# A hybrid S5, conformer and ConvFFN step on one core: an own list scheduler, and split weights kept in DRAM

## The chip, the core and the metric

The kernel runs on one core of a Trainium2 chip. The core has TensorE (PE; its weight loads are shown apart as PEld), VectorE (DVE), ScalarE (ACT), GpSimd (POOL) and SyncE (SP, which here only issues DMAs), each with an in-order stream of instructions of its own, and 16 DMA engines that move data between DRAM and SBUF. TensorE writes its products to PSUM, and DVE and ACT bring them out. The metric is the device time of one execution in microseconds (us).

## The reference, cut to what matters

A prompt of 2048 tokens and 8 single-token samples with carried state go through one layer:

```
h = RMSNorm(x); p = h @ w_in                        # 1024 -> 1536
s: S5 scan of p[:, :512], GELU, s * sigmoid(s @ w_glu)
c: p[:, 512:1024] * sigmoid(p[:, 1024:]), causal conv of 31 taps, LayerNorm, swish
x = x + RMSNorm(concat(s, c) @ w_out)
h = RMSNorm(x); u = conv3(h @ w_up)                 # 1024 -> 5632, three taps over positions
x = x + RMSNorm((silu(u_gate) * u_val) @ w_down)    # 2816 -> 1024
```

Everything is float32. The outputs are the new x and the new states.

## The kernel before, in words

Tokens are cut into six tiles of 344 (the last one is 328 and the 8 samples), and a tile's activations lie as 128 channels by 344 tokens. Two tiles make a **round**; there are three rounds (0, 1, 2), and each goes through all weights. A weight **block** is 8, 6 or 4 chunks of 128 x 128: 12 blocks of w_in (`in`), 2 of w_glu and 8 of w_out (`out`), 44 of w_up, 32 of w_down with 4 chunks and 8 of w_down with 6 chunks (`ffn`). That is 106 different blocks, used 326 times, since in the last piece of round 2 the 8 blocks of 6 chunks are read once for each of its two tiles. A number behind a name in this text is that of the round or tile; `ORDER` has the stages: in 0, in 1, a third of in 2, out 0, the rest of in 2, ffn 0, out 1, the last piece of ffn 0, ffn 1, out 2, the last piece of ffn 1, ffn 2, the last piece of ffn 2. That last piece is the 8 blocks of 6 chunks; behind out 1 and out 2 it is what TensorE can do while the norms of the next round are worked out.

For float32 accuracy each operand is split in two: H is the value in the type fp32r, L the rest of it. A product is three matmuls, W_H h_H, W_H h_L and W_L h_H (`group`). There are 12672 of them, with output `ps`, called the **main matmuls** below. A block comes from DRAM into `wraw` (`w_load_to`, L327, on SP's queue), then ACT writes `wh` (its H) and POOL writes `wlo`, wraw minus wh (`w_split_to`, L337). Each of the three tiles has three buffers (`NRAW`, `NW`). This is done for all 326 uses.

Beside the main matmuls run **tasks**, written as generators: the set-up of the S5 matrices (DVE work on tile `wk`), the S5 scan (steps on DVE in tiles ST and UR; round 0 has two, UR00 and UR016, of 16 channel groups each, and `CR` takes a scan's last state), the conv of 31 taps (DVE steps `acc<-c,V,acc`; the first 128 channels on POOL, in `cacc`), and the norms between stages (tiny matmuls `trp<-col_d,sqs` sum squares, a chain of tiny DVE steps on tile `st` takes the square root, `trp<-ident,st` turns the result back, and eight channel blocks are then scaled and added, in tiles mx and y). The **auxiliary matmuls** of the tasks, with output `trp`, stand in the same PE stream as the main ones. `split_h` makes the two halves of h that a stage reads.

The order of the program text is set by simple clocks (`clk`) that pace the tasks against the main matmuls, and operations marked "any" go to DVE or POOL by these clocks. The framework's scheduler then sets the order of each engine's stream.

At the start (`prep_first`) the tokens of tile 0 (xa, xb) are squared and summed on ACT (output `xn`), turned on PE, copied to xT, scaled on DVE by the norm and the gain V1 (`xn<-xT,V,trp`) and split into h; then tile 1 likewise.

## Time and profile before

| | |
|---|---|
| median of 3 runs | 2403.68 us (2399.62 to 2403.96) |
| span of the profiled execution | 2398.0 us |
| median minus span | 5.7 us |
| busy: PE, DVE, ACT, POOL | 2215.5, 1692.2, 1026.9, 1085.0 us |
| moved by DMA | 248.60 MB |

The span runs from the first to the last instruction of the profiled execution. The profiled execution is not one of the three that were timed, so the 5.7 us is how its span stands to their median: what lies around the span, and the scatter between executions. Matmuls overlap each other in their records, so PE busy in the whole of a stretch means that it never ran dry there. A windows view cuts the span into stages; a stage's bounds are the times at which its first and last main matmuls run.

### The profile page before, as it was taken

To read this page: it belongs to the slowest core of one execution; us is meant where nothing else is said; L and a number is where in the kernel's file an instruction comes from. 1 tells how busy PE (TensorE), PEld (TensorE's weight loads), DVE (VectorE), ACT (ScalarE), POOL (GpSimd) and SP (SyncE) were. 2 spreads that over 40 slices of the span, in tenths; PEclk is the share of its full clock that TensorE was granted. 3 is DMA by queue.
4 is the path that set the end of the run, shared out by engine and by line. 5 is a ranking of instruction groups with operands and counts; after the bars stand their busy time and mean duration, and the time that the engine had idled before them with its cause. 6 is when DMAs were issued, how large, how long until landed. Compare 5 with 4: busy or idle time off the path is not lost.

```text
span 2398.0 us, 36717 instructions
## 1 busy us (share of the span) xinstructions
PE 2215.5 (92%) x13923; PEld 2185.1 (91%) x13923; DVE 1692.2 (71%) x3156; ACT 1026.9 (43%) x1897; POOL 1085.0 (45%) x708
## 2 busy tenths in 40 slices
PE   8897788979898999999898999999997899999997
PEld 8887788979898899999888999999897899999997
DVE  8979985388789997564799896644549835445464
ACT  5666355344444234454443433345335443233345
POOL 3797443343233334444665434333537533333335
PEclk8998899989999999999999999999998999999999
DMA  7859333352342232142332322323324222222224
GB/s 222 207 146 235 105 112 114 85 140 80 90 127 83 62 86 77 58 146 79 122 133 79 89 60 65 88 91 89 107 88 145 91 64 64 86 62 63 88 84 137
DMA packets 361501, 248.60 MB, mean 104 GB/s; under 512 B 53824, under 2 KB 343352, under 8 KB 357685
## 3 DMA queue, kind: packets, MB, share of 16 engines
q1 hardware_dynamic: 318503, 218.21, 31.6%
q10 hardware_dynamic: 42470, 27.37, 4.3%
q8 instruction: 110, 1.80, 0.3%
q0 software_dynamic: 352, 0.67, 0.1%
q14 instruction: 66, 0.54, 0.1%
HBM read 197.60 MB, written 48.10 MB: 102 GB/s over the span
## 4 chain that ended last, share of the span: by engine, by line
PE 58%; DVE 29%; issue 3%; ACT 3%; DMA 1%; POOL 1%; DVEq 0%; ACTq 0%; SPq 0%; POOLq 0%
PE ps L114 56%; DVE acc L99 7%; DVE ST L82 4%; DVE UR L82 3%; DVE y L82 2%; DVE mx L99 2%; DVE mx L82 2%; PE trp L114 2%; DVE sqs L82 1%; DVE st L99 1%; DVE h L82 1%; DVE xT L99 1%; PE trp L118 1%; DVE s L99 1%; DVE acc L82 1%
## 5 line engine op out<-in xcount | busy, mean ns | idle before, releaser
L114 PE MATMUL ps<-h,wh 128*128 128x346 f32 (+3 forms) x5376 | 1310.3, 326 | 32.3 <-DVE h L82 15.7
L85 POOL TENSOR_TENSOR wlo<-wraw,wh 128x1024 fp32r<-128x1024 f32 (+2 forms) x326 | 672.1, 2063 | 931.9 <-ACT wh L75 888.5
L114 PEld LDWEIGHTS ps<-h,wh 128*128 128x128 f32 x5376 | 947.0, 192 | 39.4 <-DVE h L82 18.9
L114 PE MATMUL ps<-h,wlo 128*128 128x346 f32 (+3 forms) x2688 | 872.2, 325 | 0.0
L114 PE MATMUL ps<-f,wh 128*128 128x344 f32 (+1 forms) x2112 | 511.4, 326 | 10.5 <-DVE acc L99 7.1
L114 PEld LDWEIGHTS ps<-h,wlo 128*128 128x128 f32 x2688 | 514.7, 192 | 0.2
L99 DVE SCALAR_TENSOR_TENSOR acc<-ps,FC,acc 128x344 f32<-128x344 f32 (+1 forms) x528 | 299.9, 569 | 238.3 <-ACT acc L75 232.1
L75 ACT ACTIVATE wh<-wraw 128x1024 fp32r<-128x1024 f32 (+2 forms) x326 | 295.8, 908 | 352.0 <-PE ps L114 236.9
L114 PEld LDWEIGHTS ps<-f,wh 128*128 128x128 f32 x2112 | 372.4, 193 | 12.6 <-issue 10.0
L99 DVE SCALAR_TENSOR_TENSOR acc<-c,V,acc 128x344 f32<-128x344 f32 (+1 forms) x609 | 347.8, 571 | 9.2
L114 PE MATMUL ps<-f,wlo 128*128 128x344 f32 (+1 forms) x1056 | 343.5, 325 | 0.0
L114 PEld LDWEIGHTS ps<-f,wlo 128*128 128x128 f32 x1056 | 203.5, 193 | 0.0
L85 POOL TENSOR_TENSOR f<-acc,f 128x344 fp32r<-128x344 f32 (+1 forms) x101 | 97.4, 966 | 217.5 <-ACT f L75 214.1
L75 ACT ACTIVATE acc<-ps,FC 128x344 f32<-128x344 f32 (+1 forms) x264 | 164.7, 625 | 68.8 <-PE ps L114 65.8
L82 DVE TENSOR_TENSOR y<-y,ps 128x344 f32<-128x344 f32 (+1 forms) x192 | 96.7, 506 | 117.1 <-PE ps L114 116.6
L75 ACT ACTIVATE f<-acc 128x344 fp32r<-128x344 f32 (+1 forms) x132 | 64.3, 488 | 260.1 <-DVE acc L82 260.0
L75 ACT ACTIVATE acc<-acc 128x344 f32<-128x344 f32 (+1 forms) x132 | 64.6, 490 | 243.6 <-DVE acc L99 240.7
L82 DVE TENSOR_TENSOR msq<-msq,sq 128x344 f32<-128x344 f32 (+1 forms) x49 | 58.1, 1191 | 114.5 <-ACT sq L75 114.5
L82 DVE TENSOR_TENSOR acc<-acc,HT 128x8 f32<-128x8 f32 x44 | 65.7, 1492 | 63.2 <-ACT acc L75 57.0
L85 POOL TENSOR_TENSOR cacc<-cacc,wk 128x344 f32<-128x344 f32 x87 | 94.0, 1080 | 27.6 <-ACT wk L75 24.2
L114 PE MATMUL ps<-sHL,wh 128*128 128x344 f32 (+1 forms) x384 | 95.4, 328 | 10.5 <-ACT sHL L75 7.9
L82 DVE TENSOR_TENSOR UR<-UR,ST 128x336 f32<-128x336 f32 (+11 forms) x156 | 95.8, 616 | 0.9
(243 smaller groups left out, 2526.5 us busy)
## 6 DMA issues: line engine op xcount, KB each, us to landing
wraw<-in_w_up_dram SPq DMA_DIRECT2D x132, 512.0 KB
wraw<-in_w_down_dram SPq DMA_DIRECT2D x96, 256.0 KB
wraw<-in_w_in_dram SPq DMA_DIRECT2D x36, 512.0 KB
wraw<-in_w_out_dram SPq DMA_DIRECT2D x24, 512.0 KB
wraw<-in_w_down_dram SPq DMA_DIRECT2D x32, 384.0 KB
xTd<-xT SPq DMA_DIRECT2D x5, 1376.0 KB
xr<-xTd SPq DMA_DIRECT2D x5, 1376.0 KB
x1d<-mx SPq DMA_DIRECT2D x5, 1376.0 KB
```

What stands on the lines that cost most here:

```text
L75: nc.scalar.activation(out, in_, func, bias=bias, scale=scale)
L82: nc.vector.tensor_tensor(out, a, b, op=op)
L85: nc.gpsimd.tensor_tensor(out, a, b, op=op)
L99: nc.vector.scalar_tensor_tensor(out, a, s, b, op0=op0, op1=op1)
L114: nc.tensor.matmul(out, lhsT, rhs, start=start, stop=stop)
L118: nc.tensor.transpose(out, in_, ident_)
```

## The change

Two things come in one edit.

First, the framework's scheduler is switched off. The body runs against a recorder, which keeps every operation with its engine, its duration by a formula and the operations that it depends on. `place` then plays the program through: an engine that is free takes, of the operations that are ready, the one recorded first; DVE and POOL operations that work in SBUF exclude each other; float32 matmuls and transposes (`late`, which are the auxiliary ones) are offered 1000 ns after they are ready; all DMAs share one channel. The instructions are written in the order that comes out, and buffers are bound to the slots that the play gave them. All of them have one line number in the changed kernel, that of the helper.

Second, a block that is used again is split only at its first use. Both halves are then stored to DRAM (`wd`, from SP's queue), and later uses load them from there, straight into `wh` and `wlo`. All 106 blocks are used again, so there are 106 splits instead of 326 (66 instead of 198 with 8 chunks, 32 instead of 96 with 4, 8 instead of 32 with 6), 212 stores and 440 loads of halves instead of 220 loads of `wraw`. A block's first use lies in round 0. Besides, 29 of the 31 products `f<-acc,f` that DVE had go to POOL.

```diff
+LAG = {"pe": 170.0, "act": 95.0, "dve": 80.0, "pool": 45.0}
+SEM = 60.0
+TURN = 1000.0
...
+    def tensor_tensor(self, out, a, b, op):
+        n = self._n(out)
+        lock = not self._psum(a) and not self._psum(b)
+        if self.eng == "pool":
+            self._put("tensor_tensor", [out], [a, b], (out, a, b), dict(op=op), n * 2.17 + 178, lock=True)
+        else:
+            self._put("tensor_tensor", [out], [a, b], (out, a, b), dict(op=op), n / 0.96 + 147, lock=lock)
...
+    def scalar_tensor_tensor(self, out, a, s, b, op0, op1):
+        n = self._n(out)
+        aps = [s] if isinstance(s, View) else []
+        lock = not self._psum(a) and not self._psum(b)
+        self._put("scalar_tensor_tensor", [out], [a, b, *aps], (out, a, s, b), dict(op0=op0, op1=op1),
+                  n / 0.96 + (210 if aps else 150), lock=lock)
...
+    def matmul(self, out, lhsT, rhs, start, stop):
+        n = self._n(out)
+        r = lhsT.dtype == F32R
+        g = n / 2.4 + 14.5 if r else 2 * max(76 if n < 32 else 92 if n < 100 else 112, n / 1.2)
+        self._put("matmul", [out], [lhsT, rhs] + ([] if start else [out]), (out, lhsT, rhs),
+                  dict(start=start, stop=stop), g, done=g + LAG["pe"], late=not r)
+
+    def transpose(self, out, in_, ident):
+        g = max(62.0, self._n(out) / 1.2 + 2)
...
+        self._put("dma_start", [out], [in_], (out, in_), {}, 800.0 if self.eng == "pool" else 400.0,
+                  byte=size / (400.0 * r / (r + 230.0)), lock=self.eng == "pool")
...
+    def add(self, eng, call, outs, ins, args, kw, ns, done=None, lock=False, func=None, byte=0, late=False):
...
+        o.prio = n + self.prio
...
+        def offer(n, t):
+            o = ops[n]
+            t = max(t, rdy[n])
+            push(t + (TURN if o.late else 0.0), "ready", n)
...
+        def pick(e):
+            q = ready[e]
+            if not q:
+                return None
+            if e == "dve" and lock["pool"] > now and ops[q[0][1]].lock:
+                held = []
...
+            while t_free[e] <= now + 1e-6:
+                if e == "pool" and lock["dve"] > now + 1e-6:
+                    push(lock["dve"], "free", e)
+                    return
+                n = pick(e)
+                if n is None:
+                    return
+                o = ops[n]
...
+                o.at = now
+                seq.append(n)
+                t_free[e] = now + ns
+                if o.lock and e in lock:
+                    lock[e] = now + ns
+                if o.byte:
+                    chan = max(chan, now + ns) + o.byte
+                    fin = chan + 1900.0
+                else:
+                    fin = now + done
+                push(t_free[e], "free", e)
...
+        for n in self.place():
+            o = self.ops[n]
+            o.call(*[real(a) for a in o.args], **{k: real(a) for k, a in o.kw.items()})
...
-    nc = tc.nc
...
+    ctx.enter_context(tc.manual_schedule())
+    nc = Recorder(tc.nc)
...
+    first_use = {}
+    for n, (src, sh, key) in enumerate(wl):
+        first_use.setdefault(key, n)
+    reused = {first_use[key] for n, (_, _, key) in enumerate(wl) if n != first_use[key]}
+    staged = {n: dram.tile([128, 2, wl[n][1][0] * wl[n][1][1]], F32, f"wd{n}") for n in sorted(reused)}
...
-            src, sh = wl[n]
+            src, sh, key = wl[n]
+            if first_use[key] != n:
+                hl = halves[n] = w_tiles(n)
+                for k in range(2):
+                    nc.sync.dma_start(hl[k].bitcast(F32), staged[first_use[key]][:, k])
+                w_pos[0] += 1
+                continue
...
-            sh = wl[n][1]
-            raw = w_raw.pop(n)
-            hl = []
-            for nm in ("wh", "wlo"):
-                t = wp.tile([128, 8, 128], F32R, name=nm, tag=nm, bufs=NW)
-                hl.append(t.rearrange("p a b -> p (a b)")[:, :sh[0] * sh[1]].rearrange("p (a b) -> p a b", a=sh[0]))
-            with tc.high_priority(700 if n > 1 else 0):
-                act(hl[0], raw)
-                tt(hl[1], raw, hl[0].bitcast(F32), OP.subtract, "pool")
+            if n in halves:
+                hl = w_shaped(n, halves.pop(n))
+            else:
+                raw = w_raw.pop(n)
+                flat = w_tiles(n)
+                hl = w_shaped(n, flat)
+                with nc.first(700 if n > 1 else 0):
+                    act(hl[0], raw)
+                    tt(hl[1], raw, hl[0].bitcast(F32), OP.subtract, "pool")
+                if n in staged:
+                    for k in range(2):
...
+    nc.trace()
```

Three places show how the order moves. Rows of before have the line of their operation, those of the change the helper's; the digits after a name only number buffers. The first is ACT at the start of the program; xn, xT and h are those of tile 0 in `xn_143`, `xT_142`, `h_245` and of tile 1 in `xn_165`, and in the changed kernel names carry the tile (xn0, xn1). Before:

```order
L528 ACTIVATE xn_143,ss<-xa_137 128x1024 x2
L528 ACTIVATE xn_143,ss<-xb_138 88x1024
L75 ACTIVATE wh<-wraw 128x1024
L75 ACTIVATE st<-st 128x3
L75 ACTIVATE xT_142<-trp 128x4x128
L75 ACTIVATE xT_142<-trp 128x4x88 x2
L75 ACTIVATE wh<-wraw 128x1024
L75 ACTIVATE h_245<-xn_143 128x2x344
L75 ACTIVATE wh<-wraw 128x1024
L528 ACTIVATE xn_165,ss<-xa_159 128x1024
```

And after the change:

```order
L396 ACTIVATE xn0_277,ss_244<-xa0_240 128x1024 x2
L396 ACTIVATE xn0_277,ss_244<-xb0_253 88x1024
L396 ACTIVATE wh_311<-wraw_258 128x1024
L396 ACTIVATE st_314<-st_314 128x3
L396 ACTIVATE xn1_329,ss_246<-xa1_260 128x1024 x2
L396 ACTIVATE xn1_329,ss_246<-xb1_267 88x1024
L396 ACTIVATE wh_365<-wraw_270 128x1024
L396 ACTIVATE xT0_321<-trp_334 128x4x128
L396 ACTIVATE xT0_321<-trp_338 128x4x88
L396 ACTIVATE xT0_321<-trp_344 128x4x88
L396 ACTIVATE wh_385<-wraw_272 128x1024
L396 ACTIVATE h00_473<-xn0_277 128x2x344 x4
```

The three squares of tile 1 and one split have moved ahead of the three copies of tile 0 to xT.

The second place is DVE at the end of round 0's second scan (UR016), where CR0 is written for the second time. Before:

```order
L82 TENSOR_TENSOR UR016_2061<-UR016_2061,ST016_2062 128x16x21
L99 SCALAR_TENSOR_TENSOR acc_3157<-c0_922,V2_95,acc_3157 128x344
L82 TENSOR_TENSOR ST016_2062<-UR016_2061,PWr_100 128x16x42
L82 TENSOR_TENSOR ST016_2062<-UR016_2061,PWi_101 128x8x42 x2
L109 COPY CR0_105<-UR016_2061 128x2x8
L99 SCALAR_TENSOR_TENSOR acc_3157<-c0_922,V2_95,acc_3157 128x344
L82 TENSOR_TENSOR UR016_2061<-UR016_2061,ST016_2062 128x16x42
L99 SCALAR_TENSOR_TENSOR acc_3157<-c0_922,V2_95,acc_3157 128x344
L99 SCALAR_TENSOR_TENSOR xT5_2046<-xT5_2046,V1_94,bc_2720 128x336 x6
```

And after the change:

```order
L396 TENSOR_TENSOR ST016_3017<-UR016_2973,PWr_92 128x16x42
L396 TENSOR_TENSOR ST016_3017<-UR016_2973,PWi_93 128x8x42 x2
L396 SCALAR_TENSOR_TENSOR xT5_2358<-xT5_2358,V1_86,bc_3395 128x336
L396 TENSOR_TENSOR UR016_2973<-UR016_2973,ST016_3017 128x16x42
L396 SCALAR_TENSOR_TENSOR xT5_2358<-xT5_2358,V1_86,bc_3395 128x336
L396 TENSOR_TENSOR UR016_2973<-UR016_2973,ST016_3017 128x16x42
L396 SCALAR_TENSOR_TENSOR xT5_2358<-xT5_2358,V1_86,bc_3395 128x336
L396 COPY CR0_97<-UR016_2973 128x2x8
```

The eight scalings of xT5, which stood behind this copy, now stand between the scan's last steps. Over the whole stream up to this copy, 23 more conv steps and the eight scalings stand ahead of it: 660 instructions instead of 621.

The third place is SP's queue in the last piece of round 2 (16 blocks), around the load of xr, the residual that the end of tile 4 reads back; the rows of before begin at the seventh block, and xt is the result of the last tile. Before:

```order
L333 DMA wraw<-in_w_down_dram 128x6x128 x3
L1268 DMA xr_22490<-x1d_122 128x2752
L333 DMA wraw<-in_w_down_dram 128x6x128 x7
L1378 DMA out_dram<-xt_22186 112x512 x2
```

And after the change, from the third block on, with the rest of the blocks following in the same way:

```order
L396 DMA xr_22030<-x1d_114 128x2752
L396 DMA wh<-wd_229 128x768
L396 DMA wlo<-wd_229 128x768
L396 DMA wh<-wd_230 128x768
L396 DMA wlo<-wd_230 128x768
L396 DMA out_dram<-bgt 44x128 x2
L396 DMA wh<-wd_231 128x768
L396 DMA wlo<-wd_231 128x768
```

Where one load brought a block, there are two, one behind the other; the load of xr has moved from behind the ninth block to behind the second.

## Rows read from the trace of the kernel before

**Rows 1.** The page: span, busy time, granted TensorE clock in 40 slices, DMA.

```profile
span 2398.0 us, 36717 instructions
PE 2215.5 (92%) x13923; PEld 2185.1 (91%) x13923; DVE 1692.2 (71%) x3156; ACT 1026.9 (43%) x1897; POOL 1085.0 (45%) x708
...
PEclk8998899989999999999999999999998999999999
...
DMA packets 361501, 248.60 MB, mean 104 GB/s; under 512 B 53824, under 2 KB 343352, under 8 KB 357685
```

**Rows 2.** Windows: window, us, then busy us (count), PEclk, DMA share, GB/s.

```profile
core 0: us, PE busy (x) PEld busy (x) DVE busy (x) ACT busy (x) POOL busy (x), PEclk, DMA share, GB/s
0.00:151.00 151.00, 132.04 (x856) 128.94 (x857) 124.72 (x342) 88.69 (x158) 93.15 (x78) 0.93 0.72 194
151.00:309.00 158.00, 122.53 (x761) 119.53 (x760) 157.32 (x286) 82.53 (x158) 102.45 (x79) 0.88 0.66 167
309.00:357.00 48.00, 40.34 (x269) 39.58 (x268) 39.70 (x66) 25.76 (x37) 17.49 (x11) 0.93 0.43 121
357.00:452.00 95.00, 87.71 (x546) 85.34 (x545) 46.62 (x59) 42.56 (x80) 33.44 (x16) 0.95 0.34 100
452.00:527.00 75.00, 66.47 (x435) 66.12 (x434) 52.22 (x97) 29.07 (x54) 37.58 (x22) 0.93 0.46 116
527.00:867.00 340.00, 304.00 (x1829) 298.60 (x1828) 301.05 (x692) 139.90 (x312) 109.82 (x72) 0.95 0.34 90
...
1151.00:1222.00 71.00, 56.80 (x336) 55.68 (x335) 65.24 (x109) 32.90 (x65) 53.39 (x37) 0.86 0.40 131
1222.00:1319.00 97.00, 88.03 (x552) 85.14 (x551) 94.21 (x173) 36.77 (x65) 51.68 (x37) 0.96 0.28 89
...
1786.00:1857.00 71.00, 55.32 (x336) 53.92 (x335) 65.09 (x108) 33.27 (x65) 52.43 (x37) 0.88 0.41 135
1857.00:1951.00 94.00, 87.76 (x557) 85.90 (x555) 73.90 (x121) 37.43 (x74) 44.42 (x30) 0.95 0.24 75
1951.00:2327.00 376.00, 376.00 (x2402) 376.00 (x2401) 176.24 (x266) 131.18 (x251) 139.33 (x83) 1.00 0.26 76
2327.00:2398.00 71.00, 57.22 (x390) 54.71 (x389) 36.09 (x67) 36.83 (x66) 39.93 (x28) 0.94 0.40 125
```

**Rows 3.** Waits of PE: what for, us in total, times, longest.

```profile
PE trp L114 <- DVE sqs L82: 25.2, 4, 8.5
PE trp L114 <- ACT ST L75: 21.5, 3, 16.5
PE ps L114 <- DVE acc L99: 17.7, 12, 4.4
PE trp L118 <- DVE st L99: 16.9, 6, 5.5
```

**Rows 4.** POOL's splits by form: count, busy us, mean ns, idle before.

```profile
L85 POOL TENSOR_TENSOR wlo<-wraw,wh 128x1024 fp32r<-128x1024 f32 x198 | 486.8, 2460 | 615.4 <-ACT wh L75 576.4 <-DMA bgt<-in_x_prompt_dram 25.4 <-ACT st L75 5.8
L85 POOL TENSOR_TENSOR wlo<-wraw,wh 128x512 fp32r<-128x512 f32 x96 | 124.9, 1302 | 253.5 <-ACT wh L75 249.1 <-PE ps L114 3.8 <-PE trp L114 0.6
L85 POOL TENSOR_TENSOR wlo<-wraw,wh 128x768 fp32r<-128x768 f32 x32 | 60.4, 1888 | 63.1 <-ACT wh L75 63.0
```

**Rows 5.** Timeline at 1240 us, DVE then POOL: start, duration.

```profile
1239.86 0.16 DVE L95 TENSOR_SCALAR st<-st 86x4 int32<-86x4 int32 x1
1239.93 0.51 DVE L82 TENSOR_TENSOR acc<-acc 128x344 f32<-128x344 f32 x1
1240.36 2.38 DVE L95 TENSOR_SCALAR st<-st 86x4 int32<-86x4 int32 x1
...
1239.85 2.86 POOL L85 TENSOR_TENSOR wlo<-wraw,wh 128x1024 fp32r<-128x1024 f32 x1 [4.23 <-ACT wh L75]
```

**Rows 6.** Timeline of the start, ACT, DVE and PE.

```profile
11.42 1.29 ACT L75 ACTIVATE xT<-trp 128x512 f32<-128x512 f32 x3
...
20.62 1.04 ACT L528 ACTIVATE xn<-xa 128x1024 f32<-128x1024 f32 x1
...
19.82 0.94 PE L114 MATMUL ps<-h,wh 128*128 128x344 f32 x2 [4.25 <-ACT h L75]
```

**Rows 7.** DVE's groups by form in 0 to 357 us: count, busy us, mean ns.

```profile
L99 DVE SCALAR_TENSOR_TENSOR acc<-c,V,acc 128x344 f32<-128x344 f32 x145 | 83.2, 574 | 2.3
...
L99 DVE SCALAR_TENSOR_TENSOR xT<-xT,V,bc 128x336 f32<-128x336 f32 x8 | 9.5, 1240 | 0.0
```

**Rows 8.** Tile CR on DVE, 0 to 400 us: durations ns, first and last start.

```profile
L109 DVE COPY CR<-UR x2: 158/849/1540, 277.8 to 303.4; 128x16 f32<-128x16 f32 x2
```

**Rows 9.** Windows, as rows 2, of two shorter stretches.

```profile
200.00:250.00 50.00, 38.62 (x244) 38.02 (x243) 49.72 (x93) 35.51 (x73) 36.22 (x29) 0.90 0.91 228
...
2345.00:2365.00 20.00, 20.00 (x135) 20.00 (x134) 7.48 (x16) 12.83 (x22) 16.92 (x12) 1.00 0.60 187
```

More of the change, by code (lines that the diff above doesn't have):

```diff
@@ L42, with _atoms @@
 NORM = [1250, 750, 5000, 500]
+LAG = {"pe": 170.0, "act": 95.0, "dve": 80.0, "pool": 45.0}
+SEM = 60.0
+TURN = 1000.0
+SETS = {"Sqrt": {3}, "Gelu": {10}, "Silu": {18}, "Tanh": {0, 10, 18}}
+def _atoms(side):
+    out, group = [], None
+    for t in side.replace("(", " ( ").replace(")", " ) ").split():
+        if t == "(":
+            group = []
+        elif t == ")":
+            out.append(group)
+            group = None
+        elif group is None:
+            out.append([t])
+        else:
+            group.append(t)
+    return out
@@ new lines, in _rearranged @@
+def _rearranged(a, pattern, sizes):
+    lhs, rhs = (_atoms(s) for s in pattern.split("->"))
+    dim = dict(sizes)
+    for g, n in zip(lhs, a.shape):
+        known = 1
+        for x in g:
+            known *= dim.get(x, 1)
+        for x in g:
+            if x not in dim:
+                dim[x] = n // known
+    names = [x for g in lhs for x in g]
+    a = a.reshape([dim[x] for x in names])
+    a = a.transpose([names.index(x) for g in rhs for x in g])
+    shape = []
+    for g in rhs:
+        n = 1
+        for x in g:
+            n *= dim[x]
+        shape.append(n)
+    return a.reshape(shape)
@@ new lines, with __init__, tile @@
+class Pool:
+    def __init__(self, rec, pool, bufs):
+        self.rec, self.pool, self.bufs = rec, pool, bufs
+        self.space = pool.record.space if hasattr(pool, "record") else pool.space
+    def tile(self, shape, dt, name, tag="", bufs=None):
+        import numpy as np
+        n = bufs or self.bufs
+        key = (id(self), tag or name)
+        b = Buf(self.pool, shape, dt, {"name": name}, key, n)
+        b.space = self.space
+        b.tag = tag or name
+        self.rec.bufs.append(b)
+        if self.space == bass.MemoryType.DRAM or not tag:
+            b.real = self.pool.tile(shape, dt, name=name)
+            b.fixed = True
+        else:
+            b.fixed = False
+            self.rec.order.setdefault(key, []).append(b)
+        size = 1
+        for s in shape:
+            size *= s
+        return View(b, np.arange(size, dtype=np.int32).reshape(shape), dt, ())
@@ L53, with pool @@
 ):
[L54 to L62 removed]
+    ctx.enter_context(tc.manual_schedule())
+    nc = Recorder(tc.nc)
+    def pool(name, bufs, **kw):
+        return Pool(nc, ctx.enter_context(tc.tile_pool(name=name, bufs=bufs, **kw)), bufs)
+    const = pool("const", 1)
+    slots = pool("slots", NSLOT)
+    wp = pool("wp", 3)
+    small = pool("small", 2)
+    dram = pool("dram", 1, space=bass.MemoryType.DRAM)
+    ps_mm = pool("ps_mm", NPS, space=bass.MemoryType.PSUM)
+    ps_cv = pool("ps_cv", 1, space=bass.MemoryType.PSUM)
+    ps_tr = pool("ps_tr", 3, space=bass.MemoryType.PSUM)
     clk = {"pe": 0.0, "act": 0.0, "dve": 0.0, "pool": 0.0}
@@ L286, in cols @@
     def cols(w, k0, k1, c0, n):
-        return (w[0, k0 * 128:k1 * 128, c0:c0 + n].rearrange("(k p) f -> p k f", p=128), [k1 - k0, n])
+        return (w[0, k0 * 128:k1 * 128, c0:c0 + n].rearrange("(k p) f -> p k f", p=128), [k1 - k0, n], (id(w), k0, c0))
     part_of = []
@@ L325, with w_tiles, w_shaped @@
     w_pos = [0, 0, 0]
+    first_use = {}
[3 more added lines that the diff above has]
+    staged = {n: dram.tile([128, 2, wl[n][1][0] * wl[n][1][1]], F32, f"wd{n}") for n in sorted(reused)}
+    halves = {}
+    def w_tiles(n):
+        sh = wl[n][1]
+        hl = []
+        for nm in ("wh", "wlo"):
+            t = wp.tile([128, 8, 128], F32R, name=nm, tag=nm, bufs=NW)
+            hl.append(t.rearrange("p a b -> p (a b)")[:, :sh[0] * sh[1]])
+        return hl
+    def w_shaped(n, hl):
+        return [t.rearrange("p (a b) -> p a b", a=wl[n][1][0]) for t in hl]
     def w_load_to(i):
@@ L526, in prep_first @@
             clk["act"] += 1060
-            with tc.high_priority(1000 if i == 0 else 200):
+            with nc.first(1000 if i == 0 else 200):
                 nc.scalar.activation(junk[:sz], x[:sz], AF.Square, scale=1.0 / 32, accum_out=ss[:sz, n:n + 1])
```

286 lines of the change are left out of this document (278 added, 8 removed).

## The prediction

> **What bounds the kernel now.** I read the page first, then a table of windows by stage, then the waits of PE, and at last single groups and timelines in the stages that lose time.
>
> The page [rows 1] says that PE is busy for 2215.5 of 2398.0 us. 182.5 us are idle, and the clock row falls to 8 in places, mostly in the first quarter. So there is something to win, but not everywhere. The windows [rows 2] tell where. In 1951 to 2327 PE never runs dry at a granted clock of 1.00, the level of 2.4 GHz: 2402 matmuls in 376 us, 0.1565 us each. No order of instructions makes this stage shorter, and two stages like it are not shown. Four others lose. In 0 to 357 PE lacks 19.0, 35.5 and 7.7 us; DVE is busy for 157.3 of 158 us in its middle, so this is DVE's stage. In 357 to 527 15.8 us are lost. In 527 to 867 PE lacks 36.0 us with DVE busy for 301 of 340. Around the two places where a norm stands between out and the next ffn, PE lacks 14.2 and 9.0 (1151 to 1319) and 15.7 and 6.2 (1786 to 1951), with DVE at 65 of 71 in the first window of each and clocks of 0.86 and 0.88.
>
> The waits [rows 3] name what PE stands before. Auxiliary matmuls (`trp`), not the main ones, are where most of it waits: the three rows of this kind hold 25.2, 21.5 and 16.9 us. PE is in order, so a main matmul behind a waiting auxiliary one waits too. What is late there is work of DVE or ACT.
>
> Why DVE is slow is seen in one place [rows 5]: a step on 86x4 elements takes 0.16 us, and its like 2.38 us while POOL makes `wlo` from 1239.85 to 1242.71. POOL's splits are 486.8 + 124.9 + 60.4 = 672 us of its 1085 [rows 1, 4]. The Trainium skill, page "SBUF — State Buffer", section "Who interferes with whom", says that DVE and GpSimd share a port pair under an exclusive lock; the two rows agree.
>
> **The change, part by part.**
>
> *What is removed.* 132, 64 and 24 splits go: 132 x 2.460 + 64 x 1.302 + 24 x 1.888 = 453 us of POOL [rows 4], and as many splits on ACT. ACT is busy for 1026.9 of 2398 us [rows 1]; its time is worth nothing by itself. POOL is no bound either. What counts is how much DVE gets back in the stages that wait for DVE. Two bounds: nothing (a blocked DVE step was not on the path), or a us for each us of POOL. I take half, since the small steps of chains [rows 5] are hit hardest while conv steps beside them run at their usual time. And only later uses are freed. Round 0 splits as before: in 0, out 0, ffn 0 with its last piece.
>
> *Start, 0 to 357.* (a) On ACT, three squares and one split, 4 x 1.05 us, now stand ahead of the copies of tile 0 to xT (at 11.42 and 20.62 before) [rows 6]. The first product, at 19.82, comes at least 4.2 us later. The squares also wait for tile 1's tokens, so I take +6, bounds 0 (the stage has slack later) and +8. (b) At the end of the second scan of round 0 (at 303.4 before) [rows 8], 23 conv steps of 0.574 us and eight scalings of 1.240 us more stand ahead on DVE [rows 7]: 13.2 + 9.9 = +23. DVE has no idle time in this stage, and glu waits for this scan, so I take it in full; 0 if relief and slack swallow it. (c) The uses of in 1 and the first third of in 2 are later uses: 16 x 2.460 = 39 us of POOL, half of it is -20 (0 to -39). (d) DMA: in 0 stores 12 blocks of two halves, 12.6 MB. That is 83 GB/s more on a stage with 194 GB/s at a share of 0.72, which at a full share would be 269 [rows 2]. 277 is over 269, by 5 us, and what spills over finds a share of 0.66 in the next window. A store waits on SP for POOL's `wlo`, and behind it waits the next load of `wraw`; but that load needs the buffer that the same `wlo` frees, so it comes no later. I take 0, bound +5. Together +9, from -39 to +36.
>
> *357 to 527.* Out 0 is a first use; in 2's eight blocks are freed of 20 us of POOL. Half is 10, and PE's idle time is 15.8 us with DVE half idle. I take -5 (0 to -16).
>
> *527 to 867.* No split goes here. But DVE is idle for 39 us in a stage where PE lacks 36 and waits 17.7 us in the whole span for the conv steps of ffn (`ps` behind `acc`) [rows 2, 3]: steps stood in the wrong order. A list that takes whatever is ready fills some of this. I take -15 (0 to -36).
>
> *The two norms.* The first's last piece (1151 to 1222) still splits; the ffn behind it is freed of some 13 splits in 97 us, 32 us, and half is 16, against 23.2 us that PE lacks: -10 (0 to -23). At the second both are freed: 8 x 1.888 + 12 x 2.460 = 45 us, half 22, against 21.9 us idle and about 8 us of slow clock (0.12 of 71): -15 (0 to -30).
>
> *Saturated stages.* A block of 8 chunks serves 48 matmuls, 7.5 us, and now brings 1.05 MB: 140 GB/s where 76 at a share of 0.26 are moved now, some 290 at a full share [rows 2]. The loads are hidden. 0.
>
> *The last piece of round 2.* Here a block serves only 18 matmuls, 2.82 us, and its two halves are 786 KB: 279 GB/s. Between 2345 and 2365 the transfers made 187 GB/s at a share of 0.60, 312 at a full share [rows 9]. So they fit with a tenth to spare: 12.6 MB and 1.4 MB of xr are 45 us, just what PE takes for the 16 blocks. At the 250 GB/s that 228 at 0.91 gives [rows 9], they are 56 us, 11 over. I take +4 (0 to +13). The Trainium skill, page "DMA: Bandwidth & Descriptors", section on bandwidth, speaks against the change here: a transfer costs about 2.0 us and its bytes at 436 GB/s, and transfers under 1 MiB are far from the peak. Two halves in a row would by it be 2 x 2.9 us, 3 us more than the 2.82, so +46 us for 16 blocks. That would hold only if the transfers of a queue did not overlap.
>
> *Sum.* +9 - 5 - 15 - 10 - 15 + 0 + 4 = -32. The profiled span of 2398.0 becomes 2366, and with the 5.7 us by which the runs' median lies above it, 2372 us.
>
> **Rivals.** *A, faster: the auxiliary waits vanish.* The list places auxiliary matmuls one at a time, 1 us after the moment at which it thinks them ready, instead of in fours and eights. If its durations are right, PE no longer stands before them. They are near what rows show: it gives a conv step 344 / 0.96 + 210 = 568 ns against 574, a split of 1024 columns 2400 against 2460 [rows 4, 7]. The three `trp` rows hold 63.6 us [rows 3], so 2372 - 64 = 2308 us. Against it: chains end when they end, and an order can't hide a norm for which no other product is left.
>
> *B, no change.* The relief lies off the path, and the order gains what it loses: 2404 us, give or take 10. For it: most of the freed time, rounds 1 and 2 of ffn, lies in stages where PE is never idle.
>
> *C, slower: glu of round 0 comes late.* The list goes by recording order and knows nothing of what ends last, and it puts the conv and xT ahead of the scan's last steps. Price (a), (b) and (d) in full, +36, no relief in this stage, half of the later gains, -22, and the tail's +4: 2404 + 18 = 2422 us. It decides as soon as less than a third of the 39 us reaches DVE and the later terms come out at half. Against it: DVE's total work up to glu is only moved, and what was moved ahead isn't left for later.
>
> *D, slower: DMA is the bound.* Traffic goes from 249 MB [rows 1] to 249 + 92 + 95 = 436 (both halves of 46 MB written; 95 MB of later loads doubled). If the 12.6 MB of stores in in 0 stand in the way of the scan's and conv's transfers, that is 12.6 MB / 269 GB/s = 47 us, and the tail gives +13 instead of +4: 2372 + 47 + 9 = 2428. For it: 200 to 250 us already has a share of 0.91 [rows 9]. Against it: only a seventh of it would spill, by the sum of (d).
>
> **How the numbers follow.** Chances: the forecast (2335 to 2395) 0.45, A 0.18, B 0.13, C 0.14, D 0.10. The predicted time is the forecast's, 2372. All lower bounds together would be 2398 - 144, which isn't likely, so the range begins at A's 2308 less a little, and ends at C and D: 2300 to 2425; A's far half and D's leave some 2 in 10 outside. The forecast's own range is 2335 to 2395. About 0.2%, 5 us, is what a measurement of this kernel can tell from no change. Faster by more: 0.45 + 0.18 + 0.05 of B = 0.68. Within: 0.05 of B and the forecast's rim = 0.06. Slower: C, D and a little of B = 0.26.
>
> **What would show it.** In the new trace: the first product at 24 to 28 us; the second copy to CR after 303; POOL busy for about 630 us; DVE steps on `st` that take over 1 us gone from rounds 1 and 2; the stage 1786 to 1951 at about 150 instead of 165 us; the saturated stages unchanged at 0.1565 us a matmul; the last piece not waiting for `wh` or `wlo`. The prediction is wrong if PE waits for DMA, if `trp` waits fall to nearly nothing, or if glu of round 0 starts later than 375.

## The result, and the profile after

The changed kernel takes 2415.38 us (median of 4 runs, 2411.2 to 2419.75) against 2402.66 of the kernel before in the same comparison: a ratio of 1.0054, with a 95% interval from 1.0036 to 1.0071. It is slower by about half a per cent. The forecast was 2372 us.

The page of the changed kernel, the lines that answer to [rows 1]:

```profile
span 2409.4 us, 36723 instructions
...
PE 2237.3 (93%) x13923; PEld 2192.9 (91%) x13923; DVE 1478.4 (61%) x3124; ACT 868.7 (36%) x1678; POOL 650.2 (27%) x520
...
PEclk7999887998899989999989999999999999999999
...
DMA packets 267548, 436.32 MB, mean 181 GB/s; under 512 B 60736, under 2 KB 165944, under 8 KB 263733
```

What was to be removed is removed: POOL is busy for 435 us less and ACT for 158, 436 MB move instead of 249, and DVE is busy for 214 us less. Of these 214, 16 are the 29 products that went to POOL, and the list's order alone, a run below, already has 110 less at the same 3156 instructions. Yet the span is 11.4 us longer. PE doesn't stand idle for longer: its idle time, span minus busy time, falls from 182.5 to 172.1 us. Its busy time grows, by 22 us for the same 13923 matmuls. The place is found by counting main matmuls in both traces: the time at which a stage's first one starts can be compared, whatever the order beside it.

| main matmul that starts | before | after | difference |
|---|---|---|---|
| first of in 0 | 19.8 | 34.8 | +15.0 |
| first of in 1 | 151.2 | 155.8 | +4.6 |
| first of in 2 | 309.4 | 303.5 | -5.9 |
| first of out 0 (glu) | 357.5 | 381.3 | +23.8 |
| in 2, the rest | 451.5 | 479.0 | +27.5 |
| first of ffn 0 | 526.5 | 548.7 | +22.2 |
| 1632 matmuls into ffn 0 | 867.3 | 910.4 | +43.1 |
| first of out 1 | 1068.2 | 1111.8 | +43.6 |
| last piece of ffn 0 | 1150.6 | 1189.8 | +39.2 |
| 480 matmuls into ffn 1 | 1319.2 | 1347.1 | +27.9 |
| last piece of ffn 1 | 1786.1 | 1807.0 | +20.9 |
| 480 matmuls into ffn 2 | 1951.0 | 1961.1 | +10.1 |
| last piece of ffn 2 | 2327.1 | 2338.0 | +10.9 |
| end of the span | 2398.0 | 2409.4 | +11.4 |

Round 0 loses 43 us, the rest gives 32 back. The windows of the changed kernel, cut at its own stage bounds (columns as in [rows 2]):

```profile
0.00:156.00 156.00, 133.94 (x803) 124.03 (x804) 115.66 (x331) 80.53 (x142) 69.47 (x64) 0.90 0.86 269
156.00:303.50 147.50, 125.72 (x765) 121.09 (x764) 128.29 (x265) 77.47 (x155) 73.25 (x78) 0.89 0.81 225
303.50:381.00 77.50, 54.27 (x331) 51.50 (x331) 41.90 (x98) 28.67 (x45) 15.91 (x8) 0.79 0.55 160
...
549.00:664.00 115.00, 97.35 (x556) 95.00 (x555) 100.93 (x245) 50.04 (x111) 38.46 (x23) 0.88 0.56 175
664.00:785.00 121.00, 104.87 (x642) 102.17 (x641) 90.26 (x207) 52.10 (x114) 39.99 (x25) 0.97 0.61 198
785.00:910.00 125.00, 108.69 (x639) 105.64 (x638) 118.03 (x253) 43.50 (x92) 39.57 (x25) 0.95 0.55 176
...
1190.00:1251.00 61.00, 50.47 (x332) 49.34 (x331) 53.41 (x100) 30.42 (x60) 39.46 (x32) 0.94 0.69 244
1251.00:1347.00 96.00, 89.67 (x554) 87.71 (x555) 91.90 (x190) 30.94 (x58) 34.44 (x30) 0.93 0.41 140
...
1961.00:2338.00 377.00, 377.00 (x2402) 377.00 (x2401) 119.98 (x252) 86.29 (x186) 31.37 (x35) 1.00 0.45 147
2338.00:2409.40 71.40, 58.09 (x390) 54.74 (x388) 28.90 (x63) 26.85 (x51) 14.97 (x15) 0.94 0.63 205
```

In 303 to 381, the stretch before glu, PE lacks 23 of 77 us, and no other engine is busy for more than 42: no engine is full there, so work waits for work. In 549 to 910 PE lacks 50 us where it lacked 36 [rows 2]. The saturated stage is what it was, and the last piece has no wait for a transfer of any weight: PE's waits there are 4.6 us for ACT and 2.4 for others.

What the scan before glu waits for is read from single tiles. `rows` is the row of gains that is turned into V1, `bs` what the set-up of the S5 matrices makes from its tiles AB, CA the tiles of its last part, `Cd<-CA` their stores, `UR<-ud` the load of a scan's input (8 for each of round 0's scans). Columns: durations (least, median, most, in ns), first and last start. In the kernel before:

```profile
L118 PE MATMUL trp<-ident,rows x20: 194/197/247, 12.6 to 35.6; 1*128 1x1 f32 x8, 3*128 3x3 f32 x8, 35*128 35x35 f32 x4
L75 ACT ACTIVATE bs<-trp x8: 582/598/647, 90.9 to 110.5; 128x512 f32<-128x512 f32 x8
L945 SPq DMA_DIRECT2D Cd<-CA x4: 507/646/2138, 197.8 to 202.2; - x4
L976 SPq DMA_DIRECT2D UR<-ud x16: 303/447/1397, 164.1 to 187.2; - x16
```

And in the changed kernel, with the second copy to CR, which [rows 8] has at 303.4 (the view of `rows` ends at 60 us, with 17 of its 20 matmuls):

```profile
L396 PE MATMUL trp<-ident,rows x17: 219/240/263, 22.3 to 59.7; 1*128 1x1 f32 x8, 3*128 3x3 f32 x5, 35*128 35x35 f32 x4
L396 ACT ACTIVATE bs<-trp x8: 576/582/597, 104.0 to 144.6; 128x512 f32<-128x512 f32 x8
L396 SPq DMA_DIRECT2D Cd<-CA x4: 622/680/763, 240.9 to 259.8; - x4
L396 SPq DMA_DIRECT2D UR<-ud x16: 303/388/914, 196.2 to 271.8; - x16
L396 DVE COPY CR<-UR x2: 165/167/169, 289.0 to 329.1; 128x16 f32<-128x16 f32 x2
```

The copies to bs, which ended at 111, end at 145. The stores of CA move from 198-202 to 241-260. The loads of the second scan, which were done being issued at 187, are issued from 264 to 272, just behind CA's last store: the plan gives the tile UR016 the slot that CA0 had. The scan ends 26 us later than before. So my reason for its lateness (conv steps and scalings ahead of it on DVE) isn't what held it: its input wasn't there. In the run below that holds a tile's matmuls only once, the same 23 conv steps and seven of the eight scalings stand ahead, the input is issued by 248.7 us, and the copy comes 20 us earlier than here:

```profile
L397 DVE COPY CR<-UR x2: 164/169/174, 282.0 to 309.0; 128x16 f32<-128x16 f32 x2
```

### The profile page after: what moved, and what is told of

Same layout as the page of the kernel before. It is cut to its first block, busy times and chain, and to the rows that moved or that the text cites. A ratio compares the mean times of both kernels' runs of the same rounds, so it can differ in the third digit from the quotient of the medians.

```text
span 2409.4 us, 36723 instructions
## 1 busy us (share of the span) xinstructions
PE 2237.3 (93%) x13923; PEld 2192.9 (91%) x13923; DVE 1478.4 (61%) x3124; ACT 868.7 (36%) x1678; POOL 650.2 (27%) x520
## 2 busy tenths in 40 slices
DMA packets 267548, 436.32 MB, mean 181 GB/s; under 512 B 60736, under 2 KB 165944, under 8 KB 263733
## 4 chain that ended last, share of the span: by engine, by line
PE 61%; DVE 25%; DMA 5%; issue 3%; ACT 3%; POOL 1%; ACTq 0%; SPq 0%; POOLq 0%; DVEq 0%
PE ps L396 58%; DVE acc L396 12%; PE trp L396 3%; DVE ST L396 3%; DVE UR L396 3%; DVE mx L396 2%; DVE y L396 1%; DVE sqs L396 1%; DVE st L396 1%; DMA ad<-ya 1%; DMA xb<-in_x_prompt_dram 1%; DMA ud<-us 1%; DMA zd<-gt 1%; DVE xT L396 1%; ACT UR L396 1%
## 5 line engine op out<-in xcount | busy, mean ns | idle before, releaser
L396 PE MATMUL ps<-h,wh 128*128 128x346 f32 (+3 forms) x5376 | 1339.5, 331 | 35.4 <-ACT h L396 14.5
L396 PEld LDWEIGHTS ps<-h,wh 128*128 128x128 f32 x5376 | 953.4, 193 | 43.6 <-ACT h L396 16.3
L396 PE MATMUL ps<-h,wlo 128*128 128x346 f32 (+3 forms) x2688 | 882.4, 329 | 0.9 <-DMA wlo<-wd 0.9
L396 PEld LDWEIGHTS ps<-f,wh 128*128 128x128 f32 x2112 | 365.3, 189 | 6.7 <-ACT y L396 3.4
L396 POOL TENSOR_TENSOR f<-acc,f 128x344 fp32r<-128x344 f32 (+1 forms) x130 | 124.4, 957 | 877.5 <-ACT f L396 708.9
L396 POOL TENSOR_TENSOR wlo<-wraw,wh 128x1024 fp32r<-128x1024 f32 (+2 forms) x106 | 219.8, 2075 | 400.6 <-ACT wh L396 357.5
L396 ACT ACTIVATE wh<-wraw 128x1024 fp32r<-128x1024 f32 (+2 forms) x106 | 96.4, 911 | 117.1 <-PE ps L396 71.3
L396 DVE TENSOR_TENSOR msq<-msq,sq 128x344 f32<-128x344 f32 (+1 forms) x49 | 35.5, 725 | 141.8 <-ACT sq L396 141.8
L396 PE MATMUL ps<-cHL,wh 128*128 128x344 f32 (+1 forms) x384 | 93.6, 326 | 6.1 <-ACT cHL L396 6.1
L396 POOL TENSOR_TENSOR cacc<-cacc,wk 128x344 f32<-128x344 f32 x87 | 83.8, 964 | 45.7 <-ACT wk L396 41.8
L396 DVE TENSOR_TENSOR UR<-UR,ST 128x336 f32<-128x336 f32 (+11 forms) x156 | 88.6, 568 | 1.1
```

Source lines behind the costliest of these rows:

```text
L396: o.call(*[real(a) for a in o.args], **{k: real(a) for k, a in o.kw.items()})
```

## The experiments

All times are medians, and ratios are to the kernel before, run beside them. Its median was 2400.5 to 2404.4 us in these comparisons, so differences between runs of different comparisons are good to some 4 us. The code cuts are shortened.

**The two halves of the change, each alone.** The order without the stored halves:

```diff
+    wl[:] = [(src, sh, n) for n, (src, sh, key) in enumerate(wl)]
     first_use = {}
```

> The new order without the stored halves: every block is split at each use, as before. Theory 1 (the order loses in round 0, because auxiliary matmuls placed one at a time make the S5 set-up and with it the scan late; the stored halves only give back in the later rounds): glu of round 0 still starts near 380 us, ffn 0 ends about 40 us later than before, and the later rounds give nothing back, so 2425 to 2450 us. Theory 2 (the stores and doubled loads make SP's queue and the transfers late): glu is back at 355 to 362, ffn 0 ends within 10 us of before, 2390 to 2405 us.

The stored halves in the framework's own order are the diff's lines of `w_load_to` and `w_split_to` put into the kernel before; a load of halves is there issued one block later than one of `wraw`, when its buffer has been read:

```diff
+            if first_use[key] != n:
+                if not later:
+                    return
...
-        w_load_to(n + 3)
+        w_load_to(n + 3, False)
```

> The stored halves with the framework's own order, nothing of the list scheduler. Theory 1: round 0 as before, the two norm stages give back some 20 us together and the stretch up to glu some more: 2365 to 2385 us, faster than before. Theory 2: the delay in round 0 is here too, glu at 375 or later, so 2400 to 2420 us.

Measured: the order alone takes 2433.43 us, a ratio of 1.0130 (1.0114 to 1.0146). The stored halves alone take 2343.96 us, 0.9766 (0.9751 to 0.9781). Theory 2 falls, and of theory 1 the first part holds: the traffic that the halves bring doesn't cost what was lost, the order does. Its reason, matmuls placed one at a time, is tested below. The halves by themselves are worth 57 us, more than theory 1 gave them, where the terms of relief in my sum make 50. The windows of that run at the stretch up to glu and at the two norms:

```profile
162.00:289.00 127.00, 117.62 (x755) 116.31 (x756) 118.28 (x284) 65.11 (x134) 54.91 (x60) 0.94 0.90 248
1195.00:1281.00 86.00, 84.96 (x554) 83.27 (x553) 83.68 (x172) 27.83 (x54) 31.26 (x28) 1.00 0.49 174
1742.00:1802.00 60.00, 51.71 (x339) 50.39 (x337) 55.09 (x112) 26.78 (x56) 35.02 (x28) 0.97 0.57 198
```

In 1 takes 127 instead of 158 us, with DVE busy for 118 instead of 157 us at the same work. In 0 is longer, up to 162 us instead of 151, and by the main matmuls' starts the third of in 2 by 5 us and the first 1632 matmuls of ffn 0 by 4.

**Is it the relief of DVE?** In the framework's order with the stored halves, POOL is kept as busy as before by work that nothing reads:

```diff
+                junk = wp.tile([128, 8, 128], F32, name="junk", tag="raw", bufs=NRAW)
+                tt(junk[...], wh, wlo, OP.subtract, "pool")      # at each later use
```

> The stored halves with the framework's own order (2344), and at each of the 220 later uses POOL does a subtraction of the two halves into a tile that nothing reads, as long as the split that was removed. Left out is nothing; the work is added. Theory of the relief (what is gained is DVE's time, which POOL's splits took): nearly all is lost again, 2380 to 2405 us. Rival (the gain is the split that stood between a load and PE, and ACT's share of it): 2340 to 2360 us.

Measured: 2412.46 us, a ratio of 1.0035 (1.0023 to 1.0047). All 57 us are gone, and 8 more, which would be the price of stores and doubled loads; no run has it alone. DVE is the witness. The same stretch of in 1, and POOL's added group:

```profile
157.00:307.00 150.00, 125.44 (x756) 123.86 (x756) 148.24 (x291) 71.18 (x147) 97.58 (x81) 0.86 0.75 210
```

```profile
L85 POOL TENSOR_TENSOR junk<-wh,wlo 128x1024 f32<-128x1024 f32 x132 | 326.8, 2476 | 395.8 <-DMA wlo<-wd 390.1 <-PE ps L114 5.7
```

DVE's 118 us are 148 again, with 291 instructions in the stretch instead of 284. Nearly all of this is the same work, slowed by POOL. Over the whole span, first with the halves alone and then with POOL kept busy:

```profile
PE 2209.7 (94%) x13923; PEld 2183.5 (93%) x13923; DVE 1505.7 (64%) x3124; ACT 855.7 (37%) x1677; POOL 661.4 (28%) x520
PE 2227.2 (92%) x13923; PEld 2194.6 (91%) x13923; DVE 1660.5 (69%) x3157; ACT 851.1 (35%) x1677; POOL 1086.3 (45%) x707
```

DVE is busy for 155 us more. Of these, 17 are the 29 products, which the program gives back to DVE when POOL is busy; ACT's relief is the same in both and isn't what was gained. That the added work holds up the loads, since it reads the halves' buffers, is a rival of small size: SP waits for it for 10.7 us in all, at most 0.4 us at a time.

**What of the order costs?** First the second for which auxiliary matmuls are held back:

```diff
-TURN = 1000.0
+TURN = 0.0
```

> The changed kernel with TURN = 0, so auxiliary matmuls are offered as soon as they are ready and stand together again. Theory 1: the transposes of AB (32 of them between 99 and 141 us) draw together, the copies to bs end 10 to 30 us earlier, glu starts 10 to 20 us earlier, ffn 0 ends earlier: 2385 to 2405 us, if waits of PE for auxiliary work don't eat it. Theory 2: nothing of this moves the time, 2410 to 2420 us.

Measured: 2364.86 us, a ratio of 0.9852 (0.9838 to 0.9867): 50 us faster than the changed kernel, more than either theory gave. The first product comes at 20.4 us, glu at 367.4, and the gain goes on growing to the end: 31 us by the 1632nd matmul of ffn 0, 47 at the end of the span.

Then the way in which it is held. In the recorder a matmul into a PSUM tile waits for the one before it in the same tile, and each pays the second anew. Here only a tile's first one is held:

```diff
                 if b.last_pe is not None:
                     pre.add(b.last_pe)
+                    o.late = False
```

> The changed kernel (2415; 2365 with TURN = 0), where only the first auxiliary matmul into a PSUM tile is held back by the 1000 ns, not each one behind it. If the loss is that matmuls into one tile, which wait for each other in the recorder, pay the second one after another (8 transposes of the gain row 10 us, 4 of AB 5 us), nearly all of it comes back: 2360 to 2375 us, first product at 20 to 22 us. If it is the holding back itself, more than half of the loss stays: 2390 to 2415 us.

Measured: 2355.60 us, 0.9807 (0.9785 to 0.9829), 60 us faster than the changed kernel and 9 faster than without any hold. It isn't holding back that costs, but paying for it in a chain. The row of gains shows it in small: its first 8 matmuls stand together again from 9.7 us on. The page shows where the time comes from:

```profile
PE 2211.4 (94%) x13923; PEld 2186.5 (93%) x13923; DVE 1459.2 (62%) x3124; ACT 867.4 (37%) x1677; POOL 654.2 (28%) x520
```

With a span of 2356.9 us, PE is busy for 26 us less than in the changed kernel and idle for 27 us less. In the traces, auxiliary matmuls stand between main ones in 160 groups here, as in the kernel before, and in 503 in the changed kernel.

**The start.** The squares of tile 1, which had moved ahead of the copies of tile 0, are held back instead:

```diff
+                nc.hold = 15000.0 if i else 0.0
                 nc.scalar.activation(junk[:sz], x[:sz], AF.Square, ...)
+                nc.hold = 0.0
```

> The changed kernel with the squares of tile 1 held back by 15 us, so that they stand behind the copies of tile 0 to xT on ACT. Both theories: the first product comes at 22 to 27 us instead of 34.8. If the start is part of what is lost, all later stages move by some 8 to 12 us: 2403 to 2408 us. If it is made good by 151 us anyhow, as the trace suggests (15 us late at the first product, 5 at the end of in 0), nothing is left of it: 2411 to 2419 us.

Measured: 2433.37 us, a ratio of 1.0131 (1.0114 to 1.0148). Neither expectation came true. The copies do stand ahead of the squares, but the first product still comes at 32.4 us: the eight matmuls of the row of gains begin at 21.8 and come one by one, as in the changed kernel. Tile 1's h is later instead, and in 0 ends at 177.5 us. The start's 15 us are, but for some 2, those of the chained hold, not of ACT.

**The hold without the stored halves.** With TURN = 0, and held once:

```diff
 # the order alone, and:
-TURN = 1000.0
+TURN = 0.0
```

> The new order without the stored halves, as the run of the order alone (2433), but with TURN = 0. If the second that auxiliary matmuls are held back costs by itself, it gives here about what it gave with the stored halves (50 us, all over the span): 2378 to 2395 us. If it costs only where loads of halves wait on SP for PE, it gives little here: 2415 to 2433 us.

> The new order without the stored halves (2433 with TURN as it is, 2428 with TURN = 0), only the first auxiliary matmul into a PSUM tile held back. If the chained second costs by itself, it gives here what it gave with the stored halves (60 us): 2370 to 2395 us. If without the stored halves something else ends as late (the second scan behind the tiles CA, which POOL's splits slow), it gives 3 to 15 us: 2418 to 2430 us.

Measured: 2428.07 us (1.0097, 1.0082 to 1.0112) and 2434.01 us (1.0132, 1.0117 to 1.0147), against 2433.43 with the hold as it is. Without the stored halves the hold changes little: 5 us with TURN = 0, nothing when held once. That isn't because it has no price there. The pages of the order alone (span 2431.6 us) and of the same with TURN = 0 (2425.7):

```profile
PE 2243.8 (92%) x13923; PEld 2196.7 (90%) x13923; DVE 1582.5 (65%) x3156; ACT 1044.3 (43%) x1897; POOL 1077.7 (44%) x708
PE 2217.3 (91%) x13923; PEld 2186.9 (90%) x13923; DVE 1585.5 (65%) x3156; ACT 1043.3 (43%) x1897; POOL 1069.8 (44%) x708
```

The chained hold costs 26 us of PE's busy time here too, with 510 groups of auxiliary matmuls instead of 161. But here PE is idle for 20 us less with it (187.8 instead of 208.3), where with the halves it is idle for 21 us more (172.1 instead of 151.3 with TURN = 0). What turns that gain into a loss was tried by keeping POOL busy, now in the list's order with the halves and TURN = 0:

> The changed kernel with TURN = 0 (2365), and at each of the 220 later uses POOL subtracts the two halves into a tile that nothing reads. The work is added, nothing is left out. If what hides TURN's gain without stored halves is POOL's splits, TURN = 0 with a busy POOL is about as slow as the order alone with TURN = 0, 2428, and the 8 us that this cost in the framework's order: 2420 to 2445 us. If it is that loads of wraw, unlike loads of halves, don't wait for PE, it stays near 2365: 2360 to 2390 us.

Measured: 2446.59 us, a ratio of 1.0200 (1.0183 to 1.0217), just above what was expected if POOL's work hides the gain (2420 to 2445), and far from what was expected if the way of the loads does. PE is idle for 206.0 us, nearly as without the halves. The counterpart, POOL busy with the hold as it was, wasn't run, so that POOL's work hides it is likely, not shown.

**The late second scan.** Set-up and scans of round 0 go ahead of all else by their recording number, first with the stored halves and TURN = 0:

```diff
-                    t[1] = next(t[0])
+                    with nc.first(t[5]):           # 3000 for setup_mats and round 0's s5_part
+                        t[1] = next(t[0])
```

> The changed kernel with TURN = 0 (2365) and, on top, the set-up of the S5 matrices and round 0's scan taken ahead of all else by their recording number. If the second scan is late because the tiles CA of the set-up hold the slot that UR016 needs, CA is done by 225 instead of 248, UR016 is loaded by 235 instead of 258, glu starts by 355 instead of 367: 2345 to 2360 us. If the scan is late for want of transfers or DVE time, it changes by less than 5 us: 2360 to 2372 us.

Measured: 2367.81 us (0.9846, 0.9829 to 0.9862), no faster than without (2364.86). The mechanism is there: CA's stores end at 216 instead of 248, the second scan's load is issued by 234.4 instead of 257.7, and glu starts at 353.4 instead of 367.4. The scan itself ends only 5 us earlier (copy to CR at 315.9 instead of 320.9), so with its input in time something else holds it; what that is was not followed. And the rest of in 2 starts at 455.0 as before (455.9): behind glu, the conv's part of out 0 ends last, its first main matmul standing at 398.7 instead of 399.7. The same without the stored halves:

> The new order without the stored halves and with TURN = 0 (2428), the S5 set-up and round 0's scan taken ahead of all else. There the tiles CA were done at 263 us and UR016 was loaded up to 276, against 202 and 187 in the kernel before. If the order's loss of 25 to 30 us is this late second scan, CA is done by 230, glu starts by 370 instead of 391 and the time falls with it: 2400 to 2415 us. If another chain ends just as late behind it, as in the run with stored halves, the start of glu moves and the time doesn't: 2420 to 2432 us.

Measured: 2414.57 us (1.0051, 1.0036 to 1.0066), 13.5 us faster than without. Glu moves by 36 us, from 390.6 to 354.1, and 15 of them are left when the rest of in 2 starts (483.9 to 468.5). So the late scan is at most half of what the order costs by itself: the same edit also has in 2 start at 284.7 instead of 312.5, and how much of the gain that is wasn't taken apart.

**What the blocks of w_in give, and where the stores go.** In the framework's order, w_in split at each use as before; then the stores issued by POOL; then by ACT:

```diff
-    reused = {first_use[key] for n, ... if n != first_use[key]}
+    reused = {first_use[key] for n, ... if n != first_use[key] >= 12}
...
-                        nc.sync.dma_start(staged[n][:, k], ...)
+                        nc.gpsimd.dma_start(staged[n][:, k], ...)     # and nc.scalar
```

> The stored halves with the framework's own order (2344), but not for the 12 blocks of w_in, which are split at each use as before. By the stages of the run with all of them stored, in 0 comes back from 162 to 151 us and in 1 loses the 31 us that it gained: 2355 to 2372 us. If the stores of in 0 cost more than they give (the transfers are at 0.85 to 0.90 of their time in both stages): 2325 to 2343 us.

> The stored halves with the framework's own order (2344), the 212 stores issued by POOL, which made one of the halves just before, instead of by SP. If the 11 us that in 0 loses come from loads that stand on SP behind stores that wait, in 0 ends near 152 and the time is 2330 to 2340 us. If they come from the transfers themselves (a share of 0.85), it stays within 5 us of 2344; if issuing costs POOL and DVE more than SP's wait, it is slower, 2350 to 2370.

> The same with the stores issued by ACT. SP's loads are free of them as well, but ACT stands still until POOL has made the second half, some 2.5 us for each of 106 blocks, and what ACT brings out of PSUM waits behind it: 2350 to 2380 us. If ACT has room for it (busy for a third of the span), 2330 to 2345 us.

Measured: 2362.40 us (0.9823, 0.9808 to 0.9838); 2357.74 us (0.9809, 0.9789 to 0.9829); 2339.49 us (0.9737, 0.9715 to 0.9759). The 12 blocks of w_in are worth 14 to 18 us (by ratios or by medians), as their stages said: in 0 comes back to 151.5, in 1 ends at 308.4. Stores on POOL lose 14 us against stores on SP, most of them in in 1, which ends at 303.6 instead of 289.3. Stores on ACT have the lowest median of all runs, but the interval overlaps that of the stores on SP, and in 0 is longer with them, to 176 us: the two aren't told apart.

Last, the list's order held once, with the stores on ACT:

> The fastest form of the list order (held once, 2356) with the stores issued by ACT, as in the fastest run of all (2339). If the two gains add, 2345 to 2356 us; by the stage times the list order still loses 12 us in out 0 and 10 in ffn 0 against the framework's order, so it doesn't reach 2339 either way.

Measured: 2381.87 us (0.9909, 0.9885 to 0.9933), 26 us slower than with the stores on SP. The two gains don't add; why was not followed.

## Why the prediction was wrong

The forecast was that the order would gain and the halves give some relief. The sign was wrong because of the order.

**The relief was right, and its size nearly so.** The freed splits act through DVE, as said: with POOL kept busy the gain is gone. The evidence given for it was weaker than it looked, since the DVE step of 0.16 us in [rows 5], by its row, lies within POOL's span as well. In 1 and the third of in 2 were to gain 20 us; with the halves alone in 1 gained 31 and the third lost 5. Term (d), the stores of in 0, was put at nothing with a bound of 5 us and measured 11; with w_in not stored they are gone. That the two errors cancel is luck. The norms were to gain 10 and 15 us; the halves alone gain 16 and 14, the changed kernel 11 and 11. That a us of POOL is worth between nothing and one of DVE was right as a bound; over the whole, 453 us of POOL were worth 65 to 68 us of time (2344 against 2412).

**The step that failed is the order's, "a list that takes whatever is ready fills some of this", -15 in 527 to 867.** The stretch got 21 us longer. That is 36 of the 43 us by which the span missed its forecast; 18 more were lost ahead of it, and some 11 came back behind it. The waits of PE in this stretch show what went wrong (columns as in [rows 3]): before in 527 to 867, after in 549 to 910, and held once in 518 to 873:

```profile
PE ps L114 <- DVE acc L99: 17.7, 12, 4.4
PE trp L114 <- DVE Rs L109: 7.5, 2, 7.2
PE trp L114 <- ACT ST L75: 5.0, 2, 3.1
```

```profile
PE trp L396 <- ACT ST L396: 13.6, 2, 8.6
PE trp L396 <- DVE Rs L396: 9.0, 4, 7.0
PE trp L396 <- ACT UR L396: 6.1, 7, 1.9
PE ps L396 <- DVE acc L396: 4.8, 3, 3.2
```

```profile
PE trp L397 <- ACT ST L397: 19.4, 3, 10.0
PE trp L397 <- DVE Rs L397: 8.6, 2, 7.6
PE ps L397 <- DVE acc L397: 7.2, 6, 2.2
```

The list did fill the waits for conv steps, as said: 17.7 us became 4.8. But PE now stands before auxiliary matmuls of the S5 scan (ST, Rs, UR), 28.7 us instead of 12.5, and is idle for 50 us of the stretch instead of 36. The sum had counted one kind of wait and had no term for the wait that a new order makes. Held once, this stays (28 us, idle for 50), while the halves alone leave PE idle for 38, so some 12 of these 14 us belong to the list's order and not to the hold (42 in the order alone, 54 there with TURN = 0). The other 7 us are PE's busy time, and 6 of them go when held once. By stage, the order alone costs 37 us by glu and 49 by the 1632nd matmul of ffn 0, and gives 16 back behind it.

**Start and scan: the right place, the wrong reason.** Up to glu the forecast was +9 and 24 was measured; glu at 381 lies behind the 375 that the prediction had named as a sign of being wrong. (a) gave +6 for copies behind squares on ACT; it was 15, and the run that undid it changed the first product by 2 us. It was the row of gains, turned one matmul at a time: 8 in 0.65 us before, 8 in some 10 us after. I had seen in the order that auxiliary matmuls stand singly, and had put it down as rival A, in favour of the change. (b) priced DVE's work ahead of the scan at 23 us. The scan did end 26 us later, but for want of its input, so that the size fits is luck: the tiles CA are done late, and UR016 waits for their slot. The late copies to bs don't explain CA. With the halves alone they are as late and CA isn't; with the order alone at TURN = 0 they are early and CA is late:

```profile
L75 ACT ACTIVATE bs<-trp x8: 576/586/593, 102.9 to 139.2; 128x512 f32<-128x512 f32 x8
L974 SPq DMA_DIRECT2D Cd<-CA x4: 607/1446/4634, 198.4 to 204.5; - x4
```

```profile
L396 ACT ACTIVATE bs<-trp x8: 577/590/598, 96.9 to 115.6; 128x512 f32<-128x512 f32 x8
L396 SPq DMA_DIRECT2D Cd<-CA x4: 531/672/2187, 260.7 to 264.7; - x4
```

CA's last store comes at 202 us before and 260 after; held once it comes at 239, with TURN = 0 at 248, and with the set-up taken first besides at 216. So 12 to 21 of the 58 us go with the hold, and most of the rest with the turn at which the list takes the set-up's steps. Counting what stands ahead on one engine said nothing of the slot.

**The rivals.** A, that held and singly placed auxiliary matmuls free PE, failed: paid once for each tile the hold is harmless, paid in a chain it takes 60 of the 78 us that the halves are worth in this order (2434 to 2356 held once, 2433 to 2415 as it is). It did see something, since in the order alone the chained hold saves 20 us of idle time, but it had no term for the 26 us of busy time that this costs. B's bound, 2394 to 2414, ends just under the result, but for other reasons: two large effects of opposite sign, not none. C, glu of round 0 comes late, at 2422, is nearest to the time, and by luck: glu is late, by 24 us where C had 36, but by (b)'s mechanism, which was wrong; C had no relief ahead of glu, where DVE got back 29 us in in 1, and no loss in 527 to 867, where 21 us were lost. D fell: the halves' traffic costs 8 us in all when nothing else is gained. In the last piece, the estimate of +46 us (48 by its own terms) from the Trainium skill's fixed cost per transfer (page "DMA: Bandwidth & Descriptors", section "Anatomy of one DMA — SWDGE (gpsimd) path", which is about transfers that GpSimd issues; here SP does) doesn't come: from its first main matmul to its last it takes 50.4 us after the change and 51.5 before, and PE waits for no weight.

**Open.** What else in the list's order costs some 12 us by itself, after the late scan is mended (2414.57 against 2402.19), isn't settled. Ffn 0, with its waits for the scan, and the conv behind glu are the places. Why singly placed auxiliary matmuls lengthen PE's busy time is open too, and so is what the stores cost in 0: issued by POOL or by ACT, they don't shorten it.

## What to carry to other kernels

Take an edit of two parts apart before pricing the sum: here one part was worth -57 us and the other +31, and each alone was larger than their total. In an order made by a plan, look for waits that the plan itself imposes and that add up along a chain of dependences; and when something is late, follow what its tile's slot is waiting for, not only what stands ahead on its engine. An order that fills the wait you saw can make one that you didn't see, so list what each engine will stand before in the new order too. Relief on an engine that is no bound can be worth much if it slows the one that is, and it is measured by putting idle work back.

## What the runs showed of the hardware

The transfers went about as far as I had worked out. Columns as in [rows 2]. From shares and rates of the kernel before I had 250 to 312 GB/s as full. The changed kernel moves 315 GB/s in 90 to 120 us at a share of 1.04, which is 303 at a full share, and 270 GB/s at 0.83 within the last piece, which is 325. (A packet's whole time is counted in the window in which it starts, so a share can exceed 1.)

```profile
2357.00:2377.00 20.00, 20.00 (x133) 19.79 (x132) 6.03 (x20) 7.95 (x16) 3.31 (x4) 1.00 0.83 270
90.00:120.00 30.00, 27.88 (x178) 27.07 (x178) 29.14 (x61) 22.09 (x41) 21.86 (x20) 0.95 1.04 315
```

The packets fall from 361501 to 267548 while the bytes grow by three quarters, so the mean packet is larger; whether that is why the last piece lies above 312 was not tried.
